# A hybrid encoder layer on one core: a weight unit's low part last in the projections, the first squares pinned in SP's order, the last sums made in order of use

## The chip, the core and the metric

The kernel runs on one core of a Trainium2 chip, as one program with one launch. Five engines work side by side: TensorE (PE, matmuls, with its weight loads listed as PEld), VectorE (DVE), ScalarE (ACT), GpSimd (POOL) and SyncE (SP). In this kernel SP issues most of the loads, POOL's queue the loads that add to what is already there, ACT's queue a few others. The metric is the device time of one execution in microseconds. Three executions of the kernel before took 2008.85, 2009.45 and 2011.46 us; the median, 2009.45 us, is the time before. Times "at 53.19" are microseconds from the start of the span of one profiled execution.

## The reference, cut to what matters

A layer works on 512 tokens of 2048 channels in float32:

```python
xn = rms_norm(x, attn_norm_g)
u_val, u_gate, q, k, v = split(xn @ w_in)            # 2048 -> 1024 + 1024 + 3 * 1024
y_conv = silu(layer_norm(depthwise_conv(u_val * sigmoid(u_gate), 31 taps)))
y_na = neighborhood_attention(q, k, v, rpb)          # 16 heads of 64, 8 x 64 grid, window 8 x 16
mixed = concat(rms_norm(y_conv, conv_out_g), rms_norm(y_na, na_out_g))
x = x + mixed @ w_out                                # 2048 -> 2048
xn = rms_norm(x, ffn_norm_g)
gate, val = split(depthwise_conv(xn @ w_up, 3 taps)) # 2048 -> 2 * 5632
x = x + (silu(gate) * val) @ w_down                  # 5632 -> 2048
out = rms_norm(x, final_norm_g)
```

## The kernel before, in words

**Three matmuls for one.** The matmuls run on a reduced float32 type (fp32r), and each operand is a sum of a high and a low part. A weight unit is a tile of 128 x 1024 elements (512 KB), which serves 8 contraction steps (k) of 128. SP loads it into `raw`; ScalarE copies it, rounded, into `whi` (line 125); VectorE subtracts that from `raw`, and the rest is `wlo` (line 126). There are four buffers each for `whi` and `wlo`. The input x, transposed, is split in the same way into `xh` and `xl`, with the first norm's gain (`split_x`). `mm3` (lines 135 to 142) makes the three matmuls of one k: high by high, high by low (the input's low part), low by high, so line 142 is the first to read `wlo`, two matmuls after line 138 first reads `whi`.

**Order of the work.** The program is written as one list of weight units, `plan`. `weights()` hands out the next one, and sees to it that loads and splits of the three units behind it (`AHEAD`) have been written down by then. A scheduler (Tile) then orders the instructions of each engine by priority, which is mostly the place in the program; `shifted` moves an operation's priority, `issue_after` and `behind` tie it to another, and `pin` (`keep_in_program_order`) fixes the written order among pinned instructions of an engine. Work that goes between (statistics, attention) is written as generators, the `steps`; `tick` runs one step of them after each unit's matmuls.

**The stages.** First come the projections: eight channel blocks of the convolution group ("a" in `ORDER`), each a gate and a value block of two units each (`glu`, `project`), and eight head pairs ("q") of q, k and v blocks. The first block (`first_glu`) interleaves gate and value, matmul triple by matmul triple, in two PSUM banks; its weights come in small pieces (`piece`, `early`), pinned in order with the loads of x. `stats1` makes the first norm's factor beside this: it loads the untransposed x (`xn`) as eight tiles of 512 KB, ScalarE squares and sums each (line 306), VectorE reduces (line 310), a diagonal matrix is made, a matmul with ones (`st`, line 237) broadcasts it, and ScalarE copies the result out as `rstd` (line 239). The tiles of `xn` share the nine buffers of `raw`. In `gated` VectorE multiplies the gate block by `rstd` (line 352), ScalarE applies the sigmoid, VectorE makes the product, and 31 taps of the depthwise convolution follow on VectorE (line 363 the first, line 367 the other thirty), with a priority 600 later, so that they fill VectorE's free time.

The output projection has two halves of 16 columns, one for each group. The second half's `after` (from line 599) takes each finished column from PSUM: VectorE multiplies by the group's norm (line 602) and adds to x (`x2`), `sum_sq` adds its square to `acc2`, four transposes on TensorE (line 594, `turned`) prepare a copy for the end. After every second column the pair is scaled by the second norm's gain (line 611, tiles `b`, whose quarters are b11, b12, b21, b22) and made into seven operands (`halves`: a high part by ScalarE, line 586, and a low part by VectorE).

The up projection (44 hidden tiles) and the down projection then use a Strassen-like scheme of seven products, taken in the orders `TURN` and `TURN2`. In the up projection's `product` (line 696) the eight high matmuls of a unit, 512 columns wide, come first and the eight low ones, 256 wide, after them; product 2 uses `mm3` at 256 columns. Each finished hidden tile runs through `hidden` (among it the tile `vl`, line 710, and a SiLU). The down projection's `product2` takes a unit of weights and one operand and feeds four PSUM banks in turn with three matmuls each (lines 821 to 823); the last four units (`TAIL`) are fed bank by bank, so that the banks end one after the other.

Of the kernel before, what the change touches and what calls it, by code (L numbers as in the profile page):

```python
# [16 lines left out]
P = 128  # L17
# [55 lines left out]
def layer(ctx: ExitStack, tc: tile.TileContext, xT, xn, w_in, w_out, w_up, w_down, par, tab, g3, out):  # L73
# [70 lines left out]

    steps, asteps = [], []
# [137 lines left out]
    for k in range(U, KD):  # L283
        last = split_x(k)
    last = pin(nc.sync.dma_start(prm, par))
    for i in range(4):
        plan.append(lambda i=i: early[i])
# [6 lines left out]
    del plan[4:8]  # L294
# [5 lines left out]
    def stats1():  # L300
        part = sm.tile([P, S // P, 2], F32, tag="ss", name="ss")
        for t in range(S // P):
            for i in range(2):
                x = t4([P, D // 2], "xn")
                nc.sync.dma_start(x, xn[t * P:(t + 1) * P, i * D // 2:(i + 1) * D // 2])
                nc.scalar.activation(x, x, AF.Square, accum_out=part[:, t, i:i + 1])
            if t < S // P - 1:
                yield
        sums = sm.tile([P, S // P], F32, tag="s1", name="s1")
        nc.vector.tensor_reduce(sums, part, axis=AX.X, op=ALU.add)  # L310
        rstd.append((yield from root_steps(sums, D, "rstd1")))
# [287 lines left out]
    def after(d, ps):  # L599
# [4 lines left out]
        sum_sq(acc2, x2[d], d == 0)  # L604
        turned(d)
        if d % 2 == 0:
            return
        b = []
        for i in (d - 1, d):
            t = t2("b")  # L610
            nc.scalar.activation(t, x2[i], AF.Copy, scale=pc("g2", i))
            b += [t[:, :H], t[:, H:]]
        b11, b12, b21, b22 = b
        t = t2("t")
        t1, t2_ = t[:, :H], t[:, H:]
        nc.vector.tensor_sub(t1, b11, b12)
        nc.vector.scalar_tensor_tensor(t2_, b22, -1.0, t1, op0=ALU.mult, op1=ALU.subtract)
        t = t2("t")
        t3, t4_ = t[:, :H], t[:, H:]
        nc.vector.tensor_sub(t3, b22, b12)  # L620
        nc.vector.scalar_tensor_tensor(t4_, t2_, -1.0, b21, op0=ALU.mult, op1=ALU.subtract)
        for c in TURN:
            halves((t4_, t1, t3, b11, t2_, b21, b22)[c], c)


# [6 lines left out]
    def stats2():  # L632
        rstd2.append((yield from rsqrt_steps(acc2, D, "rstd2")))

# [50 lines left out]
    def up(f, done):  # L685

        def product(c, ps, more):
# [5 lines left out]
            else:  # L693
                for part, n in ((hi, S), (lo, H)):
                    for k in range(U):
                        i = nc.tensor.matmul(ps[:, :n], part[:, k * P:(k + 1) * P], comb[c][k][:, :n],  # L696
                                             start=part is hi and k == 0 and not more,
                                             stop=part is lo and k == U - 1, skip_group_check=more)
                        if part is hi and k == 0 and tight:
                            pin(i)  # L700
# [113 lines left out]
    def product2(c, ps, more):  # L814

        def feed(w, h, i, start, stop):
            wh, wl = w
            t, d = divmod(i, Q)
            t, d = slice(t * P, (t + 1) * P), slice(d * S, (d + 1) * S)
            tl = slice(H + t.start, H + t.stop)  # L820
            nc.tensor.matmul(ps[i], h[:, t], wh[:, d], start=start and not more, stop=False, skip_group_check=more)  # L821
            nc.tensor.matmul(ps[i], h[:, t], wl[:, d], start=False, stop=False, skip_group_check=more)  # L822
            return nc.tensor.matmul(ps[i], h[:, tl], wh[:, d], start=False, stop=stop, skip_group_check=more)  # L823
# [178 lines left out]
```

## Time and profile before

| | |
|---|---|
| median of three runs | 2009.45 us (2008.85 to 2011.46) |
| the profiled execution | 2008.65 us |
| its span in the trace | 2006.9 us |
| mean granted TensorE clock | 0.997 |
| PE busy | 1985.5 us, 99%, 10525 matmuls |
| VectorE busy | 1598.5 us, 80% |
| ScalarE busy | 1095.9 us, 55% |
| GpSimd busy | 225.8 us, 11% |
| DMA | 451.01 MB, mean 225 GB/s |

The page's second table cuts the span in 40 slices of about 50 us each and gives the busy share of each engine in tenths:

```profile
PE   9999999999999999999999999999999999999998
DVE  4994899488556888888888888888888898886765
ACT  6234433447534666566666666566666644554654
```

The projections take the first eleven slices or so, the output projection ends in the fifteenth, the down projection begins in the thirty-second. TensorE shows 9 in all slices but the last.

How to read the other lines: a row of the groups has line, engine, operation, tile written <- tiles read, partitions x elements, count, then the busy time in us and the mean of one in ns, then the engine's idle time just ahead of such instructions and what ended most of it. A matmul's duration there (389 ns) is from its start to its modelled end; matmuls overlap, and the time that one adds to the engine is the distance between starts. A row of the timeline has the start, the busy time, the engine, the line, the operation and its tiles, how many stand in the row, and in brackets the wait just ahead of it and what ended it. A row of the waits has the waiting engine, tile and line, the engine and tile it waited for, the sum in us, the number of waits and the longest. A row of the windows has the stretch and its length in us, the busy time (and number of instructions) of PE, PEld, DVE, ACT and POOL, the granted TensorE clock, the busy share of the DMA engines and the GB/s that they moved.

### The profile page before, as it was taken

The numbers are of one execution on the slowest core, as the hardware profiler recorded it, in microseconds if no ns is written. First come the engines' busy times: TensorE is split into PE (matmuls) and PEld (weight loads), VectorE is DVE, ScalarE is ACT, GpSimd is POOL, SyncE is SP. The second block draws the span as 40 slices with busy tenths as digits, with TensorE's granted clock in tenths as the row PEclk, the third lists the DMA queues.
The fourth block names the chain that finished last, engine by engine and source line by source line (L and its number), as shares of the span: only waits on it lengthen the run. The fifth ranks groups of instructions, "written<-read, shape, count | busy, mean of one in ns | idle before, by whom it ended". The sixth has DMA issues, their size and how long they took to land.

```text
span 2006.9 us, 28334 instructions
## 1 busy us (share of the span) xinstructions
PE 1985.5 (99%) x10525; PEld 1688.0 (84%) x10525; DVE 1598.5 (80%) x2296; ACT 1095.9 (55%) x1728; POOL 225.8 (11%) x310
## 2 busy tenths in 40 slices
PE   9999999999999999999999999999999999999998
PEld 7778888887788889888898988898898888888886
DVE  4994899488556888888888888888888898886765
ACT  6234433447534666566666666566666644554654
POOL 0111111111001111111111111111110400000000
PEclk9999999999999999999999999999999999999999
DMA  9677767766858888989999999999997877666563
GB/s 352 158 197 180 177 172 190 192 182 166 296 147 206 214 213 230 271 237 260 249 260 247 261 252 253 258 250 262 250 246 200 335 254 235 216 217 191 191 213 110
DMA packets 143115, 451.01 MB, mean 225 GB/s; under 512 B 15232, under 2 KB 23936, under 8 KB 141568
## 3 DMA queue, kind: packets, MB, share of 16 engines
q1 hardware_dynamic: 90608, 293.98, 43.0%
q0 software_dynamic: 42624, 148.92, 34.7%
q10 hardware_dynamic: 9744, 6.30, 1.0%
q8 instruction: 82, 1.34, 0.3%
q14 instruction: 57, 0.47, 0.1%
HBM read 430.27 MB, written 111.15 MB: 270 GB/s over the span
## 4 chain that ended last, share of the span: by engine, by line
PE 96%; DVE 2%; ACT 1%; DMA 1%; issue 0%; SPq 0%; DVEq 0%; ACTq 0%
PE pu L696 37%; PE pd L821 7%; PE pd L822 7%; PE pd L823 7%; PE pj L138 7%; PE pj L141 7%; PE pj L142 7%; PE po L138 3%; PE po L141 3%; PE po L142 3%; PE pu L141 2%; PE pu L142 2%; PE pu L138 2%; DVE y L367 1%; PE po L495 1%; PE sc L453 1%
## 5 line engine op out<-in xcount | busy, mean ns | idle before, releaser
L125 ACT ACTIVATE whi<-raw 128x1024 fp32r<-128x1024 f32 x572 | 605.4, 1059 | 709.7 <-PE pj L141 220.4
L126 DVE TENSOR_TENSOR wlo<-raw,whi 128x1024 fp32r<-128x1024 f32 x572 | 698.7, 1222 | 285.2 <-ACT whi L125 261.1
L696 PE MATMUL pu<-xc,whi 128*128 128x512 f32 x2112 | 529.8, 392 | 0.2 <-ACT pu L706 0.2
L696 PEld LDWEIGHTS pu<-xc,whi 128*128 128x128 f32 x2112 | 379.9, 189 | 68.8 <-issue 0.5
L696 PEld LDWEIGHTS pu<-xc,wlo 128*128 128x128 f32 x2112 | 288.1, 190 | 20.5
L696 PE MATMUL pu<-xc,wlo 128*128 128x256 f32 x2112 | 294.5, 282 | 0.0
L142 PE MATMUL pj<-xh,wlo 128*128 128x512 f32 x624 | 244.7, 392 | 7.1 <-DVE wlo L126 7.1
L138 PE MATMUL pj<-xh,whi 128*128 128x512 f32 x624 | 247.5, 399 | 0.0
L141 PE MATMUL pj<-xl,whi 128*128 128x512 f32 x624 | 245.0, 393 | 0.1
L821 PE MATMUL pd<-whi,ho 128*128 128x512 f32 x616 | 239.7, 389 | 0.5 <-DVE vl L710 0.5
L822 PE MATMUL pd<-wlo,ho 128*128 128x512 f32 x616 | 239.8, 389 | 0.0
L823 PE MATMUL pd<-whi,ho 128*128 128x512 f32 x616 | 239.5, 389 | 0.0
L367 DVE SCALAR_TENSOR_TENSOR y<-ch,prm,y 128x509 f32<-128x509 f32 (+14 forms) x240 | 170.0, 740 | 3.2
L142 PEld LDWEIGHTS pj<-xh,wlo 128*128 128x128 f32 x624 | 118.0, 189 | 33.0 <-DVE wlo L126 8.0
L138 PEld LDWEIGHTS pj<-xh,whi 128*128 128x128 f32 x624 | 118.0, 189 | 28.4 <-issue 3.7
L141 PEld LDWEIGHTS pj<-xl,whi 128*128 128x128 f32 x624 | 117.8, 189 | 24.3 <-issue 0.7
L821 PEld LDWEIGHTS pd<-whi,ho 128*128 128x128 f32 x616 | 115.7, 188 | 25.0 <-DVE vl L710 0.9
L823 PEld LDWEIGHTS pd<-whi,ho 128*128 128x128 f32 x616 | 115.7, 188 | 24.1
L822 PEld LDWEIGHTS pd<-wlo,ho 128*128 128x128 f32 x616 | 115.7, 188 | 24.1 <-DVE wlo L126 0.3
L194 POOL DMA_DIRECT2D ws<-in_w_down x88 | 79.4, 902 | 495.8 <-DMA ws<-ws 254.8
L643 POOL DMA_DIRECT2D raw<-in_w_up x88 | 86.1, 979 | 408.2 <-ACT vl L709 133.1
L138 PE MATMUL pu<-xc,whi 128*128 128x256 f32 x352 | 99.8, 284 | 1.4 <-ACT xc L586 1.4
(185 smaller groups left out, 2526.0 us busy)
## 6 DMA issues: line engine op xcount, KB each, us to landing
raw<-in_w_up SPq DMA_DIRECT2D x220, 512.0 KB, 7.2
ws<-in_w_down POOLq DMA_DIRECT2D x132, 512.0 KB, 7.4
raw<-in_w_up POOLq DMA_DIRECT2D x88, 512.0 KB, 8.5
raw<-ws SPq DMA_DIRECT2D x88, 512.0 KB, 3.4
raw<-in_w_in SPq DMA_DIRECT2D x78, 512.0 KB, 4.8
raw<-in_w_down SPq DMA_DIRECT2D x66, 512.0 KB, 4.2
ws<-ws POOLq DMA_DIRECT2D x44, 512.0 KB, 7.5
raw<-in_w_out SPq DMA_DIRECT2D x32, 512.0 KB, 4.9
```

The lines of the kernel that those rows point to most:

```text
L125: i = nc.scalar.activation(hi[:, :n], raw[:, :n], AF.Copy)
L126: j = nc.vector.tensor_sub(lo[:, :n], raw[:, :n], hi[:, :n].bitcast(F32))
L138: i = nc.tensor.matmul(ps, hi[:, a], mh, start=start, stop=False, skip_group_check=more)
L141: nc.tensor.matmul(ps, hi[:, a], ml, start=False, stop=False, skip_group_check=more)
L142: return nc.tensor.matmul(ps, lo[:, a], mh, start=False, stop=stop, skip_group_check=more)
L194: nc.gpsimd.dma_start(wsum[c][k], w_down[k, {1: A21, 2: A11, 4: A11, 6: A12}[c]], accum_op=ALU.add, max_dma_last_dim=ROW)
L367: nc.vector.scalar_tensor_tensor(y[:, a:b], h[:, a + j - PAD:b + j - PAD], prm[:, o + j:o + j + 1], y[:, a:b], op0=ALU.mult, op1=ALU.add)
L643: nc.gpsimd.dma_start(a[c], w_up[f, q2], accum_op=ALU.add)
L696: i = nc.tensor.matmul(ps[:, :n], part[:, k * P:(k + 1) * P], comb[c][k][:, :n], start=part is hi and k == 0 and not more, stop=part is lo ...
L821: nc.tensor.matmul(ps[i], h[:, t], wh[:, d], start=start and not more, stop=False, skip_group_check=more)
L822: nc.tensor.matmul(ps[i], h[:, t], wl[:, d], start=False, stop=False, skip_group_check=more)
L823: return nc.tensor.matmul(ps[i], h[:, tl], wh[:, d], start=False, stop=stop, skip_group_check=more)
```

## The change

It has four parts.

1. In `project` and in `out_half` a new helper, `group`, takes the place of `mm3`: the sixteen matmuls of a unit that read `whi` (high by high and high by low for each of 8 k) come first, the eight that read `wlo` last. In the up projection one product of one hidden tile (`f == 0 and c == 3`, the first) gets its sixteen matmuls sorted by k, high and low in turn; all others stay.
2. The two units of the second gate block, and the eight loads of `xn` with their squares, are written down at the head of the program, pinned, in a fixed order: unit, four tiles of `xn`, unit, four tiles of `xn`. The load of the parameters (`prm`) is pinned behind them instead of ahead. `stats1` keeps three empty steps and then reduces.
3. In `after`, for every pair of columns, the scaling by the gain comes straight behind the addition, each of the seven operands is made in the order in which the first products use them (3, 2, 4, 5, 1, 0, 6), directly behind the sum that it needs, and squares and transposes of the pair come behind. The transposes run for two columns at a time, one column later than before, and the last column's move into `stats2`.
4. In the down projection `feed` goes through a unit's twelve matmuls by kind: high by high for the four banks, then the operand's low part by high for the four banks, then the low weights for the four banks, so each matmul writes another bank than the one ahead of it. The last four units are fed per bank, by kind over the four units.

The diff, cut to its core:

```diff
+    def group(ps, ws, ms, first, last):
+
+        for k, ((hi, _, wk), (mh, ml)) in enumerate(zip(ws, ms)):
+            hi = hi[:, wk * P:(wk + 1) * P]
+            nc.tensor.matmul(ps, hi, mh, start=first and k == 0, stop=False)
+            nc.tensor.matmul(ps, hi, ml, start=False, stop=False)
+        for k, ((_, lo, wk), (mh, _)) in enumerate(zip(ws, ms)):
+            i = nc.tensor.matmul(ps, lo[:, wk * P:(wk + 1) * P], mh, start=False, stop=last and k == len(ws) - 1)
+        return i
...
-        last = split_x(k)
+        split_x(k)
+    squares = sm.tile([P, S // P, 2], F32, tag="ss", name="ss")
+    for u in range(2):
+        raw, i = raw_unit(w_in[NC_ + 1, :, u * U * P:(u + 1) * U * P], U * P)
+        pin(i)
+        for t in range(2 * u, 2 * u + 2):
+            for i in range(2):
+                x = t4([P, D // 2], "xn")
+                pin(nc.sync.dma_start(x, xn[t * P:(t + 1) * P, i * D // 2:(i + 1) * D // 2]))
+                if t == 2 * u and i == 0:
+                    w = parts(raw, U * P)
+                    pin(w[2])
+                    pin(w[3])
+                    early.append(w[:2])
+                pin(nc.scalar.activation(x, x, AF.Square, accum_out=squares[:, t, i:i + 1]))
     last = pin(nc.sync.dma_start(prm, par))
-    for i in range(4):
+    for i in range(len(early)):
...
-    del plan[4:8]
+    del plan[6:12]
...
     def stats1():
-        part = sm.tile([P, S // P, 2], F32, tag="ss", name="ss")
-        for t in range(S // P):
...
+        for _ in range(3):
+            yield
...
-            for k in range(U):
-                kk = u * U + k
-                m = mm3(ps, w, k, xs[kk][0], xs[kk][1], kk == 0, kk == KD - 1)
+            m = group(ps, [(*w, k) for k in range(U)], xs[u * U:(u + 1) * U], u == 0, u == KD // U - 1)
...
-            for k in range(U):
-                i = mm3(ps, w, k, m[k][0], m[k][1], k == 0, k == U - 1)
+            i = group(ps, [(*w, k) for k in range(U)], m, True, True)
...
-        sum_sq(acc2, x2[d], d == 0)
-        turned(d)
+        t = t2("b")
+        nc.scalar.activation(t, x2[d], AF.Copy, scale=pc("g2", d))
+        bs[d % 2] = t[:, :H], t[:, H:]
         if d % 2 == 0:
             return
...
+        halves(b11, 3)
+        nc.vector.tensor_sub(t3, b22, b12)
+        halves(t3, 2)
         nc.vector.tensor_sub(t1, b11, b12)
         nc.vector.scalar_tensor_tensor(t2_, b22, -1.0, t1, op0=ALU.mult, op1=ALU.subtract)
-        t = t2("t")
...
+        halves(t2_, 4)
+        halves(b21, 5)
+        halves(t1, 1)
         nc.vector.scalar_tensor_tensor(t4_, t2_, -1.0, b21, op0=ALU.mult, op1=ALU.subtract)
...
+        halves(t4_, 0)
+        halves(b22, 6)
+        for i in (d - 1, d):
+            sum_sq(acc2, x2[i], i == 0)
+        for i in (d - 2, d - 1):
+            if i >= 0:
+                turned(i)
...
         rstd2.append((yield from rsqrt_steps(acc2, D, "rstd2")))
+        turned(KD - 1)
...
-                for part, n in ((hi, S), (lo, H)):
-                    for k in range(U):
...
+                turns = [(part, n, k) for part, n in ((hi, S), (lo, H)) for k in range(U)]
+                if f == 0 and c == 3:
+                    turns.sort(key=lambda a: a[2])
...
-        def feed(w, h, i, start, stop):
...
+        def feed(got, banks, start, stop):
+
+            for kind in range(3):
+                for i in banks:
+                    t, d = divmod(i, Q)
+                    d = slice(d * S, (d + 1) * S)
+                    for j, ((wh, wl), h) in enumerate(got):
+                        o = H if kind == 1 else 0
+                        w = wl if kind == 2 else wh
+                        m = nc.tensor.matmul(ps[i], h[:, o + t * P:o + (t + 1) * P], w[:, d],
...
         for j in range(n):
-            w, h = weights()
-            for i in range(2 * Q):
-                m = feed(w, h, i, j == 0, j == NK - 1)
-            tick(m)
+            tick(feed([weights()], range(2 * Q), j == 0, j == NK - 1))
...
             for i in range(2 * Q):
-                for j, (w, h) in enumerate(got):
-                    feed(w, h, i, False, j == NK - n - 1)
+                feed(got, [i], False, True)
```

More of the change, by code (lines that the diff above doesn't have):

```diff
@@ L300, in stats1 @@
     def stats1():
-        part = sm.tile([P, S // P, 2], F32, tag="ss", name="ss")
-        for t in range(S // P):
[L303 to L308, printed above, removed]
+        for _ in range(3):
+            yield
         sums = sm.tile([P, S // P], F32, tag="s1", name="s1")
-        nc.vector.tensor_reduce(sums, part, axis=AX.X, op=ALU.add)
+        nc.vector.tensor_reduce(sums, squares, axis=AX.X, op=ALU.add)
         rstd.append((yield from root_steps(sums, D, "rstd1")))
```

36 lines of the change are left out of this document (12 added, 24 removed).

## The prediction

> **What bounds the kernel now.** I read the page first, then the waits, then windows and the order of time at each place where TensorE (PE) stood still.
>
> ```profile
> span 2006.9 us, 28334 instructions
> PE 1985.5 (99%) x10525; PEld 1688.0 (84%) x10525; DVE 1598.5 (80%) x2296; ACT 1095.9 (55%) x1728; POOL 225.8 (11%) x310
> L142 PE MATMUL pj<-xh,wlo 128*128 128x512 f32 x624 | 244.7, 392 | 7.1 <-DVE wlo L126 7.1
> ...
> L821 PE MATMUL pd<-whi,ho 128*128 128x512 f32 x616 | 239.7, 389 | 0.5 <-DVE vl L710 0.5
> ...
> L823 PE MATMUL pd<-whi,ho 128*128 128x512 f32 x616 | 239.5, 389 | 0.0
> ```
> ```profile
> PE pj L142 <- DVE wlo L126: 7.1, 2, 3.8
> ```
>
> TensorE is busy for 99% of the span, so only its stalls and its extra work can be won or lost. The waits put 7.1 us on two places, both in the projections, both a low part (`wlo`) that VectorE had not yet written. In order of time:
>
> ```profile
> 51.83 0.39 PE L138 MATMUL pj<-xh,whi 128*128 128x512 f32 x1
> ...
> 53.19 0.39 PE L138 MATMUL pj<-xh,whi 128*128 128x512 f32 x1
> ...
> 57.16 0.50 PE L142 MATMUL pj<-xh,wlo 128*128 128x512 f32 x1 [3.35 <-DVE wlo L126]
> ...
> 61.83 0.40 PE L138 MATMUL pj<-xh,whi 128*128 128x512 f32 x1
> ```
> ```profile
> 101.99 0.39 PE L138 MATMUL pj<-xh,whi 128*128 128x512 f32 x1
> ...
> 106.38 0.80 PE L142 MATMUL pj<-xh,wlo 128*128 128x512 f32 x1 [3.78 <-DVE wlo L126]
> ...
> 109.80 0.40 PE L141 MATMUL pj<-xl,whi 128*128 128x512 f32 x1
> ```
> ```profile
> 7.30:30.50 23.20, 22.45 (x94) 17.12 (x93) 15.93 (x23) 18.26 (x28) 0.00 (x0) 1.00 1.03 392
> 57.16:61.90 4.74, 4.74 (x14) 3.74 (x15) 4.74 (x6) 0.00 (x0) 0.00 (x0) 0.64 0.45 131
> 106.40:109.70 3.30, 3.30 (x8) 2.62 (x9) 3.30 (x4) 0.00 (x0) 0.00 (x0) 0.52 0.62 186
> 713.10:714.55 1.45, 0.08 (x2) 0.02 (x1) 1.28 (x4) 0.93 (x4) 0.92 (x1) 1.00 0.74 253
> ```
>
> From 51.83 to 53.19 are 6 matmuls: 0.2267 us each. From 53.19 to 61.83 are 15 (3.40 us) in 8.64 us, so 5.24 us are lost; from 101.99 to 109.80 are 10 (2.27 us) in 7.81 us, 5.54 us lost. That is 10.78 us and not 7.1: the windows (the third column from the right is the granted clock) show 0.64 and 0.52 just after each stall. The 1.37 us stall at 713 was granted 1.00. So a long wait is paid about one and a half times, a short one once.
>
> **The change, part by part.** First, the squares. The parameter load (336 KB) and one 512 KB unit move on SP's queue from ahead of the last square's load to behind it.
>
> ```profile
> 24.41 1.06 ACT L125 ACTIVATE whi<-raw 128x1024 fp32r<-128x1024 f32 x1 [1.40 <-DMA raw<-in_w_in]
> ...
> 32.33 1.06 ACT L125 ACTIVATE whi<-raw 128x1024 fp32r<-128x1024 f32 x1 [0.28 <-DMA raw<-in_w_in]
> ```
> ```profile
> 38.61 0.16 DVE L310 TENSOR_REDUCE s<-ss 128x4 f32<-128x8 f32 x1 [3.96 <-ACT xn L306]
> ...
> 41.12 1.22 DVE L126 TENSOR_TENSOR wlo<-raw,whi 128x1024 fp32r<-128x1024 f32 x1
> 47.18 0.69 DVE L352 TENSOR_TENSOR gate<-pj,rstd 128x512 f32<-128x512 f32 x1 [4.84 <-ACT rstd L239]
> ```
> ```profile
> 45.65 0.87 PE st L237 x2
> ```
>
> Between the two landings lie six loads of 512 KB: 1.32 us each. So the last square lands 2.2 us earlier, its sum comes at about 36.6 instead of 38.61, the diagonal at 39.1 instead of 41.1. In the built order of the changed kernel the broadcast matmul (`st`) stands behind 48 matmuls of the second gate pair instead of 66: those begin where the window 7.30:30.50 above ends, so it runs at 30.5 + 48 x 0.2267 = 41.4, 2.3 us after its diagonal, not at 45.65. `rstd` and with it the gates are 4.2 us earlier: 42.9 for 47.18. What lies behind it now: the third and fourth units of that pair are needed at 42.3 and 47.7 and land, after squares and parameters, at about 37.5 and 38.9.
>
> Second, the low parts last. Units of 24 matmuls (5.44 us) follow each other from 53.19 in both kernels. A low part is then needed 16 matmuls (3.63 us) into its unit, not after 2.
>
> ```profile
> 55.89 2.35 DVE L126 TENSOR_TENSOR wlo<-raw,whi 128x1024 fp32r<-128x1024 f32 x2
> 58.16 0.73 DVE L367 SCALAR_TENSOR_TENSOR y<-ch,prm,y 128x501 f32<-128x501 f32 x1
> ...
> 82.49 9.29 DVE L367 SCALAR_TENSOR_TENSOR y<-ch,prm,y 128x509 f32<-128x509 f32 x14
> 91.69 0.69 DVE L419 TENSOR_TENSOR q<-pj,rstd 128x512 f32<-128x512 f32 x1
> 92.29 7.94 DVE L367 SCALAR_TENSOR_TENSOR y<-ch,prm,y 128x502 f32<-128x502 f32 x12
> ...
> 105.10 2.36 DVE L126 TENSOR_TENSOR wlo<-raw,whi 128x1024 fp32r<-128x1024 f32 x2
> ```
>
> From start to start a tap costs 0.655 us (9.20 for 14), a multiplication 0.60, a split 1.135 (2.27 for 2). First stall: the gates' chain ahead of the split begins 4.2 us earlier and holds one operation less, so the split starts at about 51.3 for 55.89 and ends at 52.5; needed at 56.8. The stall goes (between 0 and, if only the order changed, 0.3 us).
>
> Second stall: VectorE works without pause from 64 to 105 and stays late. In the new order it starts the split of the sixth unit when the second has been read (four buffers), 53.19 + 2 x 5.44 + 0.2 = 64.3. From there to the split that stalled stand 3 splits, 44 taps, 5 multiplications and one first tap (0.45): 3.4 + 28.8 + 3.0 + 0.45 = 35.65. The split runs from 99.95 to 101.2. TensorE asks for it in its ninth unit, 53.19 + 8 x 5.44 + 3.63 = 100.34. A wait of 0.9 us remains, 1.05 us with the slower restart, and by the row at 713.10 no clock is lost. Bounds: 0 and the 5.54 us of before; I take 1.05, the queue being added up from this very stretch. Gain of both: 10.78 - 1.05 = 9.7 us. In the other projections the low part was never waited for, so there the order is worth 0. High parts are read out 8 matmuls earlier, which frees ScalarE only.
>
> Third, the hand-over to the up projection.
>
> ```profile
> 712.88 0.28 PE L142 MATMUL pu<-xc,wlo 128*128 128x256 f32 x1
> 714.53 0.39 PE L138 MATMUL pu<-xc,whi 128*128 128x256 f32 x1 [1.37 <-ACT xc L586]
> ...
> 717.05 0.28 PE L142 MATMUL pu<-xc,wlo 128*128 128x256 f32 x1
> 717.49 2.11 PE L696 MATMUL pu<-xc,whi 128*128 128x512 f32 x8 [0.17 <-ACT pu L706]
> ```
> ```profile
> 707.98 0.69 DVE L602 TENSOR_TENSOR oa<-po,rna 128x512 f32<-128x512 f32 x1
> ```
> ```profile
> 712.52 0.71 ACT L611 ACTIVATE b<-x,prm 128x512 f32<-128x512 f32 x1
> ```
>
> A 256-column matmul steps 0.12, so 1.53 and 0.32 are lost: 1.85 us. Afterwards, counted from the last output matmul: VectorE multiplies at 0.9 (a prepared sum of weights holds it that long), splits weights to 2.7, adds to 3.4, ScalarE scales to 4.1, VectorE subtracts, ScalarE and VectorE make the pair's first operand (`b11`) by 5.0. TensorE, with 8 transposes (0.9), 3 clearing matmuls (0.7), 7 high and low pairs sorted by k (2.4) and 5 short matmuls (0.6), asks at 4.9. The squares now stand behind these: `acc2` is ready at 10.4, its matmul is due at 10.5; the diagonal at 13.9 is due at 15.2. I leave 0.2 us: gain 1.65, bounds 0 (a new wait as long as the old) and 1.85.
>
> Fourth, the transposes of the second output half go in pairs.
>
> ```profile
> 634.41 0.60 PE L594 MATMUL trx<-ident,x 128*128 128x128 f32 x4
> ...
> 646.42 0.60 PE L594 MATMUL trx<-ident,x 128*128 128x128 f32 x4
> ```
> ```profile
> 123.63 0.40 PE L142 MATMUL pj<-xh,wlo 128*128 128x512 f32 x1
> 123.87 1.04 PE L441 MATMUL trv<-ident,vw 128*128 128x128 f32 x8
> ...
> 124.98 0.39 PE L141 MATMUL pj<-xl,whi 128*128 128x512 f32 x1
> ```
>
> A pair of columns lasts 12.01 us, 48 matmuls of it 10.88: two groups of 4 cost 1.13. Eight transposes in a row behind a finished unit cost 1.35 - 2 x 0.2267 = 0.9. Over 7 pairs that is 1.6 us; bounds 0 and 1.7. I take 1.6.
>
> Fifth, the down projection: the same 1848 matmuls, each in another bank than the one ahead. L821 always came behind a change of bank, L823 never: 389 ns both, so 0. The wait at its start (0.5 by L821) stays. The built order puts a weight split ahead of the last hidden tile's activation there, which I price at 0.2 us lost, up to 1.1. [...]
>
> Sum: 9.7 + 1.65 + 1.6 - 0.2 = 12.75 us. The profiled execution took 2008.65 us (1.75 beside its span), so 1995.9; the median of the three runs is 0.8 above it, 2009.45, and gives **1996.7**.
>
> **The rivals.**
> (a) The squares come no earlier, since SP's issues wait for free buffers. Then the split at 55.89 still meets its 56.8 nearly, but VectorE's queue begins 4.6 us later and loses its pauses: the second low part comes at about 103.9, 3.5 us late, long enough for the half clock of 106.40 (1.6 us). Against it: ScalarE waited for these loads by DMA at 24.41 and 32.33, so transfer order rules. 9.7 falls to 5.7: 2000.7.
> (b) The wait stays short, but the scheduler's other orders bring one or two new ones in attention or at the down projection's start, 2 to 3 us: 1999.5. For it: ScalarE's and VectorE's orders shift everywhere a little.
> (c) The other side: changing bank at every matmul costs. It would need 12.75 us / 1848 = 7 ns a matmul to eat the gain, and 9 ns to be slower by 4 us: 2013. Against it stand L821's 389 ns.
> [...]
>
> **How the numbers follow.** Forecast 0.78, (a) 0.08, (b) 0.07, (c) 0.03, (d) 0.01, and 0.03 for a gain of which only the last parts hold (2005 to 2009). 0.2% (4 us) is what a measurement here can tell. The forecast's own range: from 1994.6 (no wait left, all upper gains, and the runs' scatter of 0.6) to 1999.0 (second wait of 2 us, no gain from transposes). With (a), (b) and the runs' scatter (the slowest is 2.0 over the median, of which I take 1.3): 1994.5 to 2002.0. Faster 0.92, within 0.2% 0.04, slower 0.04.
>
> **What would show it.** The chain must hold `rstd` at 42 to 43, no wait near 53 to 57, one wait near 100 of under 1.5 us with the clock at 1.00 behind it; pairs of output columns at 11.78 us; no wait over 0.4 us in the up projection's first 10 us; down projection matmuls at 389 ns. Wrong would make it: `rstd` past 45, a `wlo` wait over 3 us, or a granted clock under 1.00 after 1580.

## The result, and the profile after

The changed kernel takes 1994.59 us (median of six executions, 1994.55 to 1995.20); the kernel before, run beside it, 2009.49 us (2008.85 to 2014.89). The ratio, into which every execution of both goes (their means are 1994.74 and 2010.55 us), is 0.9921, with a 95% interval of 0.9909 to 0.9934: faster, by 14.9 us from median to median. The forecast was 1996.7. The median lies at the very edge of the stated range (1994.5 to 2002.0), and the median before times the ratio, 1993.6, lies below it: the gain was larger than forecast, and larger than the range allowed for.

From the page of the changed kernel, the lines that answer to those of before:

```profile
span 1992.8 us, 28315 instructions
PE 1979.3 (99%) x10525; PEld 1685.3 (85%) x10525; DVE 1596.1 (80%) x2296; ACT 1097.6 (55%) x1728; POOL 225.7 (11%) x310
L846 PE MATMUL pd<-whi,ho 128*128 128x512 f32 x1232 | 305.1, 389 | 0.5 <-DVE vl L731 0.5
L152 PE MATMUL pj<-xh,wlo 128*128 128x512 f32 x608 | 150.4, 389 | 0.8 <-DVE wlo L126 0.8
```

TensorE has as many matmuls as before and is busy 6.2 us less; of 7.1 us of waits on low parts in the projections 0.8 is left. The places where it stood still, in order of time (ScalarE, VectorE and TensorE of the changed kernel):

```profile
42.40 0.60 ACT L249 ACTIVATE rstd<-st 128x512 f32<-128x512 f32 x1 [1.94 <-PE st L247]
```
```profile
43.02 0.69 DVE L368 TENSOR_TENSOR gate<-pj,rstd 128x512 f32<-128x512 f32 x1 [1.12 <-ACT rstd L249]
...
51.71 1.22 DVE L126 TENSOR_TENSOR wlo<-raw,whi 128x1024 fp32r<-128x1024 f32 x1
...
64.25 1.23 DVE L126 TENSOR_TENSOR wlo<-raw,whi 128x1024 fp32r<-128x1024 f32 x1 [1.14 <-ACT whi L125]
...
99.97 2.35 DVE L126 TENSOR_TENSOR wlo<-raw,whi 128x1024 fp32r<-128x1024 f32 x2
```
```profile
56.74 1.52 PE L152 MATMUL pj<-xh,wlo 128*128 128x512 f32 x6
...
100.04 0.39 PE L150 MATMUL pj<-xl,whi 128*128 128x512 f32 x1
101.23 2.11 PE L152 MATMUL pj<-xh,wlo 128*128 128x512 f32 x8 [0.81 <-DVE wlo L126]
```

`rstd` comes at 42.40 and the gates begin at 43.02, not at 47.18. The first low part is ready at 52.9 (51.71 and 1.22 us of work) and read at 56.74: no wait. The second is read at 101.23, 1.19 us behind the matmul ahead of it, which is 0.97 more than a step of 0.2267. The granted clock is 1.00 from 4.8 us to the last 5 us of the span.

A way to place the gain is to take the matmul with the same number, counted from the start, in both profiled executions. Rows at the borders of units and stages, start in us (the last row is the end of the span):

```
matmul   before    after   earlier by   what lies between it and the row above
   240    63.91    58.56      5.35      first low-part stall
   480   123.87   114.06      9.80      second low-part stall
  2040   434.35   424.56      9.79      projections, attention
  2880   599.42   588.97     10.45      last projections, first output half
  3720   765.81   751.80     14.01      second output half, hand-over, first up units
  8640  1571.05  1557.04     14.01      up projection
  9000  1651.25  1637.50     13.75      down projection's start
 10440  1977.65  1963.90     13.75      down projection
   end  2006.89  1992.81     14.08      last units, norm, writes
```

### The profile page after: what moved, and what is told of

It is laid out like the page before. It is cut to its first block, busy times and chain, and to the rows that moved or that the text cites. A ratio compares the mean times of both kernels' runs of the same rounds, so it can differ in the third digit from the quotient of the medians.

```text
span 1992.8 us, 28315 instructions
## 1 busy us (share of the span) xinstructions
PE 1979.3 (99%) x10525; PEld 1685.3 (85%) x10525; DVE 1596.1 (80%) x2296; ACT 1097.6 (55%) x1728; POOL 225.7 (11%) x310
## 4 chain that ended last, share of the span: by engine, by line
PE 96%; DVE 2%; DMA 1%; ACT 0%; issue 0%; SPq 0%; DVEq 0%; ACTq 0%
PE pu L718 37%; PE pd L846 21%; PE pj L149 7%; PE pj L152 7%; PE pj L150 7%; PE po L149 3%; PE po L150 3%; PE po L152 3%; PE pu L142 2%; PE pu L141 2%; PE pu L138 2%; DVE y L383 1%; PE sc L469 1%; PE po L511 1%; PE trp L497 1%; DMA raw<-in_w_in 0%
## 5 line engine op out<-in xcount | busy, mean ns | idle before, releaser
L846 PE MATMUL pd<-whi,ho 128*128 128x512 f32 x1232 | 305.1, 389 | 0.5 <-DVE vl L731 0.5
L718 PE MATMUL pu<-xc,wlo 128*128 128x256 f32 x2112 | 295.6, 282 | 0.0
L149 PE MATMUL pj<-xh,whi 128*128 128x512 f32 x608 | 241.5, 397 | 0.0
L150 PE MATMUL pj<-xl,whi 128*128 128x512 f32 x608 | 237.7, 391 | 0.0
L383 DVE SCALAR_TENSOR_TENSOR y<-ch,prm,y 128x510 f32<-128x510 f32 (+14 forms) x240 | 169.8, 739 | 3.1
L846 PE MATMUL pd<-wlo,ho 128*128 128x512 f32 x616 | 165.0, 389 | 0.0
L152 PE MATMUL pj<-xh,wlo 128*128 128x512 f32 x608 | 150.4, 389 | 0.8 <-DVE wlo L126 0.8
L152 PEld LDWEIGHTS pj<-xh,wlo 128*128 128x128 f32 x608 | 114.0, 188 | 24.9 <-DVE wlo L126 1.2
L138 PE MATMUL pu<-xc,whi 128*128 128x256 f32 x352 | 99.6, 283 | 0.0
L142 PE MATMUL pu<-xc,wlo 128*128 128x256 f32 x352 | 99.6, 283 | 0.0
L141 PE MATMUL pu<-xc,whi 128*128 128x256 f32 x352 | 99.6, 283 | 0.0
```

The source lines that it names most:

```text
L138: i = nc.tensor.matmul(ps, hi[:, a], mh, start=start, stop=False, skip_group_check=more)
L141: nc.tensor.matmul(ps, hi[:, a], ml, start=False, stop=False, skip_group_check=more)
L142: return nc.tensor.matmul(ps, lo[:, a], mh, start=False, stop=stop, skip_group_check=more)
L149: nc.tensor.matmul(ps, hi, mh, start=first and k == 0, stop=False)
L150: nc.tensor.matmul(ps, hi, ml, start=False, stop=False)
L152: i = nc.tensor.matmul(ps, lo[:, wk * P:(wk + 1) * P], mh, start=False, stop=last and k == len(ws) - 1)
```

## The experiments

The theory: TensorE's two stalls come from VectorE's lateness; the pinned squares start VectorE's queue 4.2 us earlier, the new order gives each low part 14 matmuls more, and only both together take the stalls away. The rivals: one of the two alone does it; the gain is elsewhere.

### The low parts last, alone

The kernel before with `group` in `project` and `out_half`:

```diff
-            for k in range(U):
-                kk = u * U + k
-                m = mm3(ps, w, k, xs[kk][0], xs[kk][1], kk == 0, kk == KD - 1)
+            m = group(ps, [(*w, k) for k in range(U)], xs[u * U:(u + 1) * U], u == 0, u == KD // U - 1)
```

> The kernel before with the low parts last in the two projections alone. If VectorE's lateness and the place of the low part together set the two stalls (my theory): the broadcast matmul stands behind 70 matmuls of the second gate pair, at about 46.4, so rstd comes later than before, the first split ends near 57.9 and is asked for at 56.8: a wait of about 1.1 us; the second low part comes at about 104.7 and is asked for at 101.5: a wait of about 3.2 us with up to 1.6 us of half clock behind it. Of 10.8 us about 4.9 are won: 4.9 us faster than before. If the order alone is what removes the stalls (rival): no wait over 0.5 us at either place, 10.8 us faster. If the order does nothing without the squares: both waits stay over 3 us, less than 1 us faster. Transposes and hand-over stay as before.

Measured: 2006.16 us against 2010.25, 4.1 us less, ratio 0.998 (0.9971 to 0.9989). Its TensorE rows at the two places:

```profile
58.37 1.88 PE L152 MATMUL pj<-xh,wlo 128*128 128x512 f32 x7 [0.41 <-DVE wlo L126]
...
106.28 0.97 PE L152 MATMUL pj<-xh,wlo 128*128 128x512 f32 x3 [4.10 <-DVE wlo L126]
```

The first wait is short, the second is as long as before (4.1 us; 3.2 were expected), with a granted clock of 0.50 behind it (107.50 to 110.80, last section). By matmul 480 this kernel is 3.15 us ahead of the kernel before, not 9.8: the order alone isn't enough, and it does something. The rest was not expected: 0.70 us are won between matmuls 1900 and 2600, while the hand-over wait is longer than before (1.8 us for 1.4) and the transposes ahead of it wait 0.9 us; 1.0 us is lost between 2880 and 3720.

### The squares first, alone

The kernel before with the pinned units, loads and squares, and the parameters behind them.

> The kernel before with the pinned first loads and squares alone. My theory: rstd at 42 to 43, the first wait gone (split ready near 52.9, asked for at 53.6); the second low part is ready near 101 but asked for at 97.2, two matmuls into its unit: a wait of about 3.8 us with up to 1.6 us of half clock: 5.4 us faster than before, the second stall as large as before. Rival, the earlier squares are what counts and the order only rearranges: both waits under 1.5 us, 9 to 11 us faster. Rival, the squares come no earlier: rstd past 45, no gain.

Measured: 2003.54 us against 2010.25, ratio 0.9958 (0.9943 to 0.9973). Windows of this kernel around its one low-part stall, and two later ones (columns as in the windows above: stretch and length, busy time of PE, PEld, DVE, ACT, POOL, granted clock, DMA share, GB/s):

```profile
97.20:100.50 3.30, 1.06 (x5) 0.57 (x4) 3.30 (x5) 1.06 (x1) 0.24 (x1) 1.00 0.77 127
100.55:103.90 3.35, 3.35 (x9) 2.59 (x8) 3.35 (x5) 0.00 (x0) 0.00 (x0) 0.50 0.88 221
701.30:704.60 3.30, 1.67 (x10) 1.49 (x11) 3.30 (x5) 1.58 (x3) 0.04 (x1) 1.00 0.00 0
```

The first stall is gone, the second is a wait of 2.2 us with a granted clock of 0.50 behind it (second row, 3.35 us). By matmul 480 the kernel is 6.06 us ahead. 3.8 us were expected for the second wait: between the sixth unit's split and this one stand 41 taps and 4 multiplications in VectorE's queue here, and I had counted the 44 and 5 of the changed kernel. With the run above: 3.15 and 6.06 make 9.2 of the 9.8 us that both together bring. So the two gains nearly add up; neither part alone takes both stalls away, but only 0.6 us of the gain needs them together. In this execution 2.5 us are lost again near 703 (third row); that wait has its own run below.

### The sums in order of use, alone

The kernel before with the new `after`, `turned(KD - 1)` in `stats2` and the sorted product.

> The kernel before with the sums in order of use, the paired transposes and the one sorted product alone. My theory: both low-part waits in the projections as before; a pair of output columns lasts 11.78 instead of 12.01 us (1.6 us over seven pairs); no wait over 0.2 us in the first 10 us of the up projection instead of 1.4 and 0.2 (1.85 us): 3.5 us faster. Rival, the squares put behind the sums make a new wait as long as the old at the second norm's matmul: 1.6 us faster, with 1 to 2 us of wait on acc2.

Measured: 2005.73 us against 2010.25, ratio 0.9972 (0.9961 to 0.9983). In the trace the hand-over wait on `xc` is gone; one of another kind is left:

```profile
PE pu L703 <- ACT pu L712: 0.4, 1, 0.4
```

From matmul 2880 to 3720 it gains 3.25 us, what the prediction's third and fourth step summed to (1.65 and 1.6), and the changed kernel gains 3.56, without that 0.4 us wait. The low-part waits are those of before (7.1 us), as expected. What they cost is not: by matmul 480 this execution is 1.29 us behind the kernel before; its mean granted clock is 0.996, that of the kernel before 0.997. Its seven executions lie within 2.0 us (2004.87 to 2006.87); those of the runs with one of the other parts alone spread over 4.7, 4.7 and 7.9 us.

### Each matmul in another bank, alone

> The kernel before with the down projection's matmuls by kind, each in another bank, alone. My theory: matmuls stay at 389 ns and start every 0.2267 us, granted clock 1.00 throughout the stage, total within 0.5 us of before. Rival, changing bank costs 7 ns a matmul: 13 us slower. [...]

Measured: 2010.05 us against 2010.25, ratio 0.9993 (0.9983 to 1.0004). From matmul 9000 to 10440 both kernels take 326.40 us. A group and a window of its page:

```profile
L825 PE MATMUL pd<-whi,ho 128*128 128x512 f32 x1232 | 305.1, 389 | 0.5 <-DVE vl L710 0.5
```
```profile
1600.00:1990.00 390.00, 390.00 (x1722) 323.03 (x1721) 301.47 (x496) 205.59 (x307) 3.23 (x6) 1.00 0.65 212
```

Changing the bank at each matmul costs nothing here, and the clock stays at 1.00. 0.25 us are lost at the stage's start, as in the changed kernel. From median to median the four parts alone gain 4.1, 6.7, 4.5 and 0.2 us, 15.5 in sum, and all four together 14.9.

### The transposes one column at a time

The changed kernel with

```diff
         if d % 2 == 0:
+            if d:
+                turned(d - 1)
             return
...
-        for i in (d - 2, d - 1):
-            if i >= 0:
-                turned(i)
+        turned(d - 1)
```

> The changed kernel with its transposes made for one column at a time again, one column late. If the pairing is what shortened the columns (my theory): a pair of output columns lasts 12.01 us for 11.78, the span is 1.6 us longer than the changed kernel's, nothing else moves by over 0.2 us. Rival, the columns are shorter because of the order of high and low parts around them: 11.78 stays, no difference.

Measured, in one execution: 1997.57 us, span 1995.8, 3.0 us over the changed kernel's, but not where it was expected. Rows of TensorE, of this kernel first, then of the changed kernel and of the kernel before:

```profile
630.46 0.60 PE L609 MATMUL trx<-ident,x 128*128 128x128 f32 x4
630.81 0.48 PE L149 MATMUL po<-mbh,whi 128*128 128x512 f32 x1
...
642.28 0.60 PE L609 MATMUL trx<-ident,x 128*128 128x128 f32 x4
```
```profile
635.70 1.03 PE L609 MATMUL trx<-ident,x 128*128 128x128 f32 x8
636.49 0.48 PE L149 MATMUL po<-mbh,whi 128*128 128x512 f32 x1
...
647.48 0.71 PE L609 MATMUL trx<-ident,x 128*128 128x128 f32 x5
```
```profile
636.93 0.40 PE L138 MATMUL po<-mbh,whi 128*128 128x512 f32 x1
637.31 0.63 PE L594 MATMUL trx<-ident,x 128*128 128x128 f32 x4
637.70 0.47 PE L141 MATMUL po<-mbl,whi 128*128 128x512 f32 x1
...
646.42 0.60 PE L594 MATMUL trx<-ident,x 128*128 128x128 f32 x4
646.78 0.48 PE L138 MATMUL po<-mbh,whi 128*128 128x512 f32 x1
```

Two columns take 11.82 us here (630.46 to 642.28), 11.78 in pairs, 12.01 before. So the pairing is worth 0.04 us and the place 0.19: four transposes between two units delay the next matmul by 0.36 us (646.42 to 646.78, or 630.46 to 630.81); in the midst of a unit, behind a high matmul and ahead of one that reads the same weights, a group costs 0.54 (0.77 from 636.93 to 637.70, less a step of 0.2267). The 3 us are lost later. Two waits of 0.9 us stand between 690 and 730 us. The earlier one, and the rows of ScalarE, VectorE and TensorE that lead to it:

```profile
PE pu L703 <- DVE oa L617: 0.9, 1, 0.9
```
```profile
694.65 0.42 ACT L601 ACTIVATE xc<-b 128x256 fp32r<-128x256 f32 x1 [1.58 <-DMA xt<-xt]
...
696.23 0.69 DVE L617 TENSOR_TENSOR oa<-po,rna 128x512 f32<-128x512 f32 x1
...
696.97 0.50 PE L703 MATMUL pu<-xc 128*128 128x512 f32 x1 [0.86 <-DVE oa L617]
```

ScalarE waits 1.58 us to write an operand (`xc`), until the write of a transposed column (`xt`) to DRAM is done; VectorE, which needs that operand's high part, stands still for 1.02 us; it takes the last column but one from PSUM only at 696.23, and TensorE waits 0.86 us for that. The changed kernel has no such wait of `xc`. It is the wait that has its own run below; whether the place of the transposes brings it on, one execution can't tell. What else makes up the 3 us (eight transposes fill TensorE there in the changed kernel, here four, elsewhere; the second wait stands at 721.71, on the first hidden tile) no run here separates. So the 3 us can't be read as the price of transposes that aren't paired.

### The first product unsorted

```diff
-                if f == 0 and c == 3:
+                if False:
```

> The changed kernel with the first up product unsorted (eight high matmuls, then eight low ones). My theory: the last k's operand is asked for 0.6 us earlier than it is ready: a wait of 0.4 to 0.7 us on xc at the hand-over, span longer by as much. Rival, the order of the sums alone removes the wait: no difference over 0.1 us.

Measured, in one execution: 1994.32 us, span 1992.5. Between matmuls 2880 and 3720 it is 0.02 us slower than the changed kernel. The rival was right. The matmul that needs the late operand is the same and starts at nearly the same time (699.29, and 699.42 in the changed kernel); ahead of it the scheduler put twelve short matmuls of the next product instead of five:

```profile
697.63 0.28 PE L138 MATMUL pu<-xc,whi 128*128 128x256 f32 x1
...
699.29 0.50 PE L718 MATMUL pu<-xc,whi 128*128 128x512 f32 x1
```

### Buffers of their own for the transposed columns

The kernel before, on one chip, scattered from 2007.84 to 2015.85 us in 22 executions; the changed kernel stays within 0.65 us. The traces of the squares alone and of the banks alone, both with the old `after`, show a wait that the profiled execution of before doesn't have; of the one with the banks alone, TensorE and ScalarE between 690 and 720 us:

```profile
PE trx L594 <- DVE x L603: 2.0, 1, 2.0
```
```profile
ACT xc L586 <- DMA xt<-xt: 2.3, 1, 2.3
```

An operand (`xc`) that ScalarE wants to write waits for the write of a transposed column (`xt`) to DRAM; behind it VectorE's queue, and the next transposes, stand still. Both tiles come from one pool of 75 buffers. The run takes four of them for `xt` alone:

```diff
-NT = 75
+NT = 71
...
-        r = t2("xt").rearrange("p (t k) -> p t k", t=S // P)
+        r = tp.tile([P, S], F32, tag="xt", name="xt", bufs=4).rearrange("p (t k) -> p t k", t=S // P)
```

> The kernel before with four buffers of their own for the transposed columns xt, taken from the pool that they shared with the operands xc (75 to 71 buffers). If the 2 us wait of the transposes near 705, which some executions of the kernel before show and its profiled one doesn't, comes from an xc that takes over a buffer which the write of xt is still reading (my theory): no wait of ScalarE on that write and none of over 0.3 us by the transposes, and the median 0.5 to 2 us under that of the kernel before, with fewer executions over 2012. Rival, VectorE or ScalarE is late there for another reason: the wait shows again, median within 0.5 us.

Measured: 2008.71 us against 2009.83, ratio 0.999 (0.9982 to 0.9998). Its twelve executions lie between 2007.03 and 2009.90, the seventeen of before between 2008.32 and 2016.95. Eight of the seventeen are over 2010, none of the twelve. Neither wait is in its trace, which alone shows little, since the one trace of before doesn't have them either. The times bear the theory out: 1.1 us of the median and the executions over 2010 go with the shared buffers. How many executions of the kernel before meet that wait can't be read, since only one has a trace. A scatter of 2.9 us stays. One source of it shows in the traces: the low-part stalls don't cost the same in each, with waits of the same length (7.1 us, the longest 3.8, in this trace and in that of before); the second one costs 0.9 us more in this run's trace.

### Where 0.66 us in attention come from

The changed kernel with the low parts last in the first 20 units only; the later units of the projections go k by k again (the output projection, against what the text below says, was left as changed).

```diff
+            if weights.at < 20:
+                m = group(ps, [(*w, k) for k in range(U)], xs[u * U:(u + 1) * U], u == 0, u == KD // U - 1)
+            else:
+                for k in range(U):
+                    kk = u * U + k
+                    m = mm3(ps, w, k, xs[kk][0], xs[kk][1], kk == 0, kk == KD - 1)
```

> The changed kernel with the low parts last only as far as the unit that waited at 101 (20 units); the later projection units and the output projection's first and second half take high and low parts k by k again. My reading of the 0.66 us between 445 and 505 that the sum did not foresee: they come from the later units' order, so the two 0.5 us waits (st on s, trp on s) return and the span is 0.5 to 0.9 us longer, the first 110 us unchanged. Rival, they come from the earlier squares and shorter queue of taps: nothing changes before 600 us, within 0.2 us.

Measured: 1995.54 us, ratio 0.9921 (0.9903 to 0.9938). Two waits of the kernel before are back in its list; first the list of before, then that of this run:

```profile
PE trp L481 <- ACT s L469: 0.5, 1, 0.5
...
PE st L382 <- DVE s L461: 0.5, 1, 0.5
```
```profile
PE trp L502 <- ACT s L490: 0.5, 1, 0.5
...
PE st L403 <- DVE s L482: 0.5, 1, 0.5
```

Between matmuls 1900 and 2600 it loses 0.68 us to the changed kernel, and behind matmul 480 nothing elsewhere. The gain there belongs to the order of the later units.

### A version with an early split

The wait that is left at 101.2 is VectorE's queue of taps, so a version takes taps from ahead of that split: its unit is written down one unit earlier, and pinned ahead of the third block's taps. Two small edits at the down projection's start go with it (the operand's low part third in six units, and the free second bank of a tile kept).

```diff
+        if len(made) == 16:
+            pin(j)
...
-        while len(made) < min(at + 1 + AHEAD, len(plan)):
+        while len(made) < min(at + 1 + AHEAD + (at == 12), len(plan)):
...
-            nc.vector.tensor_scalar(y, h, ...)
+            first = nc.vector.tensor_scalar(y, h, ...)
+            if i == 2:
+                pin(first)
...
-            for kind in range(3):
+            for kind in kinds:          # (0, 2, 1) in the first six units, else range(3)
...
-    a = four(True)
+    a = [two[:, 0], two[:, 1]] + [psa.tile([P, S], F32, tag="tr", name="pd", bufs=2) for _ in range(2)]
```

> The changed kernel with three small edits: the weights of the unit whose low part is still waited for at 101.2 are written down one unit earlier, and its split is pinned on VectorE ahead of the third block's taps; the down projection's first bank group keeps the tile whose second bank is free, so that six more matmuls can run ahead of the bank that waits for the last hidden tile; in the first six units there the operand's low part is read third, not second. If VectorE's queue of taps sets the remaining wait in the projections (my theory): no wait over 0.2 us near 100, 1.1 us won; at the down projection's start the 0.64 and 0.19 us stalls go: 1.9 us less than the changed kernel, a span of about 1990.9. Rival, the wait only moves: taps held back make VectorE late for a later unit, a wait of 1 us or more between 100 and 130, no gain.

Measured: 1993.02 us, ratio 0.9913 (0.9899 to 0.9926), span 1990.8. VectorE of this version:

```profile
80.11 1.22 DVE L126 TENSOR_TENSOR wlo<-raw,whi 128x1024 fp32r<-128x1024 f32 x1
```

The split runs at 80.1 instead of 99.97, the matmuls that read it begin at 99.75, the wait is gone (1.10 us between matmuls 400 and 480), and nothing waits in its place. At the down projection's start 0.26 us are won by the new order; the 0.64 us stall stays: the spare bank didn't help. Another 0.52 us lie before 33 us, in the first loads, which none of the edits touches; that the span came out as expected is luck. So the version ran once more, beside the changed kernel:

> The version with the early split once more, on the same chip as the changed kernel: 1.4 us (its gains near 101 and at the down projection's start) to 2 us under the changed kernel's median. If the gain seen was scatter of the first loads: within 0.5 us.

> The changed kernel once more, beside the version with the early split and the kernel before. The same span as before within 0.6 us (1992.2 to 1993.4), executions within 1 us of each other, about 15 us under the kernel before; the kernel before again scatters over 5 us or more.

Measured: 1993.42 us (1992.77 to 1993.72) against 1994.67 (1993.88 to 1995.08) of the changed kernel, 1.25 us less; both against 2009.89 (2009.47 to 2017.63) of the kernel before, ratios 0.9909 (0.9892 to 0.9927) and 0.9916 (0.9900 to 0.9931). 1.4 were expected as the least: 0.13 us are lost at the hand-over, by a 0.2 us wait on `xc` that the first execution of this version didn't have. No execution of this version took as long as the shortest of the changed kernel. It beats both kernels, the changed one by little. The changed kernel's own span is 1992.9 us, as expected, its executions lie within 1.2 us (1 was expected), and those of before scatter over 8 us again.

## Why the prediction failed, and what of it held

**What failed.** The mechanism of the two stalls held; the sum around it was too small, and its range too narrow below. Two steps failed. The first is a term put at nothing: "In the other projections the low part was never waited for, so there the order is worth 0." It is worth 0.66 us. The second is the step from the profile to the median: "the median of the three runs is 0.8 above it, 2009.45, and gives 1996.7." It gave the changed kernel the scatter of the kernel before, and the runs showed that this scatter goes with the change. The range's lower end counted all upper gains of the named terms and the scatter, and nothing for what wasn't named. Of the 3.1 us between 1996.7 and 1993.6, the terms of the sum are 1.3, the carried distance 0.8, and 1.0 the slower executions of the kernel before that ran beside the changed one.

**The sum, step by step**, forecast against the same matmul's start in both traces: the two low-part stalls 9.7, measured 9.80. Hand-over and second output half 1.65 + 1.6 = 3.25, measured 3.56 (1.77 and 1.79, divided at matmul 3380, the first of the up projection). The down projection's start -0.2, measured -0.26. Last projections and attention 0, measured 0.66. The last units and writes 0, measured 0.33. The sum was 12.75 and is 14.08.

**First and second step: right, in place and size.** The broadcast was put at 41.4 and runs at 41.34; the gates were put at 42.9 and begin at 43.02; the split of the first stall was put at 51.3 and starts at 51.71; the sixth unit's split at 64.3, it starts at 64.25; the late split at 99.95, it starts at 99.97; the wait at 0.9, 1.05 with the restart, and it is 0.97 and 0.11. The queue could be added up so closely because VectorE has no pause between the last two splits. The clock stayed at 1.00. The runs with one part alone bear the two steps out: 3.15 and 6.06 us, and 0.6 us more with both.

**The term of 0.** The premise holds, the conclusion doesn't. With the order of a unit, what the scheduler puts between its matmuls moves too, and two waits of 0.5 us on the attention's results went. They stood in the list of waits of before; I had costed only the waits on low parts. The run with k by k in the later units shows that they belong to this order.

**Third step: right in its reading of the wait, 0.12 us too small.** The wait went as worked out. The 0.2 us kept back shrank to 0.15 us, a wait of the second norm's matmul (`st` on `acc`). But the sort by k, which I had counted as the reason that TensorE asks later, is worth 0.02 us: the scheduler fills the time with other matmuls.

**Fourth step: right in the length of a pair, wrong in its reason.** The columns last 11.78 us as forecast; but not because transposes go in pairs. They went from the midst of a unit to its end. I counted seven pairs, 1.6 us, and put 1.7 as the upper bound; the whole half gains 1.79.

**Fifth step: right.** No cost of the banks, and a small stall at the start, on the low part of an operand (`ho`). TensorE's weight load waits for it, and ScalarE's rows there give a reason why it is late:

```profile
PEld pd L846 <- DVE ho L800: 0.3, 1, 0.3
```
```profile
1567.87 1.06 ACT L125 ACTIVATE whi<-raw 128x1024 fp32r<-128x1024 f32 x1 [2.88 <-PE pd L846]
1568.83 0.80 ACT L760 ACTIVATE uy<-g,prm 128x512 f32<-128x512 f32 x1
```

The weight split (1567.87) stands ahead of the last hidden tile's activation (`uy`), as the forecast said; VectorE has one more split there too, at 1568.96. The operand's low part is made at 1572.75, 1.3 us later against the matmuls than in the kernel before, and asked for only two matmuls later. That the splits make it late is read from the order of the rows; no run here moves them.

**The last part: not in the sum.** 0.33 us at the end: 0.17 of it in the last units by kind (the run with the banks alone has the same 0.17), the rest behind the last instruction of ScalarE, in the landing of the last write; from that instruction to the end of the span it is 4.5 to 5.1 us in the traces here, in no order by kernel.

**The scale to the median.** I added the 0.8 us by which the median of three stood over the profiled execution to the forecast too. But the profiled execution of before was one of its fast ones. Beside the changed kernel, the mean of before (2010.55) is another 1.1 us over its median, with one execution at 2014.89; the executions of the changed kernel lie within 0.65 us, and its profiled one (1994.58) is at their median. Two sources of scatter show in the runs, and neither shows in the traces of the changed kernel: the wait on the shared buffers (1.1 us of the median, by the run with buffers of their own; of the four parts alone only the sums in order of use have executions close together), and the low-part stalls, which with the same 7.1 us of waits cost 0.9 us more (buffers of their own) and 1.29 us more (sums in order of use) than in the trace of before. ScalarE of the changed kernel still waits once for a write of `xt` (0.6 us), but TensorE does not wait behind it. That the two are all of the scatter isn't shown.

**The rivals.** (a) was excluded by `rstd` at 42.40. (b) brought no new waits; those of the scheduler's other orders went the other way. (c) fell: the matmuls stayed at 389 ns. (d), a lowered clock in the down projection, shows in no trace or run: in the window of the run with the banks alone, 1600 to 1990, the granted clock is 1.00 and TensorE busy for 390.00 us of 390.00, and in the changed kernel's trace the clock is 1.00 up to 1987.9.

## What to carry to other kernels

A split that stays late can be found by adding up the queue of the engine that makes it: the starts of its operations, from the last pause on, gave the new wait to within 0.1 us here. Where an order changes inside every unit, look at all waits in the list, also those on other tiles, since whatever is placed between the units moves with it. And where a kernel's executions scatter while others agree within 0.1%, the one trace you have may lack a wait, or show one that costs more in another (0.9 and 1.29 us more here): ask which part of the scatter the change removes, count it as a gain of its own rather than carry the distance to the median over, and let the range hold it.

## What the runs showed of the hardware

**The granted clock behind the stalls.** In the trace of the kernel before, the granted clock was 0.50 from 58.39 to 61.80 and from 106.17 to 109.59, 3.41 us each, and 1.00 between the two. The first began 1.2 us behind the end of a wait of 3.35 us (57.16), the second 0.2 us ahead of the end of one of 3.78 us (106.38). Behind the wait of 1.37 us that ended at 714.53 it stayed at 1.00, and behind that of 0.81 us in the changed kernel (to 101.23) too. Windows of the kernel with the banks alone (the last holds the wait on `xt` of the run above), and of that with the low parts last alone:

```profile
52.50:55.80 3.30, 1.37 (x7) 0.79 (x5) 3.30 (x6) 3.16 (x4) 0.94 (x1) 1.00 0.49 78
55.90:59.20 3.30, 1.97 (x5) 1.58 (x6) 3.30 (x5) 0.00 (x0) 0.00 (x0) 0.50 0.42 76
59.30:62.70 3.40, 3.40 (x10) 2.62 (x9) 3.40 (x5) 0.00 (x0) 0.00 (x0) 0.50 0.74 190
707.90:711.20 3.30, 1.57 (x9) 1.43 (x10) 3.30 (x5) 1.48 (x3) 0.00 (x0) 1.00 0.00 0
```
```profile
104.10:107.40 3.30, 1.12 (x5) 0.94 (x6) 3.30 (x5) 1.06 (x1) 0.00 (x0) 1.00 0.04 10
107.50:110.80 3.30, 3.30 (x9) 2.51 (x9) 3.30 (x4) 0.00 (x0) 0.51 (x1) 0.50 0.84 259
```

The rows at 52.50 and 104.10, and at 97.20 of the run with the squares, have 1.93, 2.18 and 2.24 us idle (length less PE's busy time), and 0.50 behind them. The rows at 707.90, and at 701.30 of the run with the squares, have 1.73 and 1.63 us idle; the matmuls behind them start 0.23 us apart (seven from 711.48 to 713.07 and from 704.78 to 706.38), the step at full clock, where those behind the first stall of before started 0.43 us apart (58.43 to 61.41) at 0.50. The length of a wait alone didn't decide here: 2.24 us ahead of 100.18 had 0.50 behind it, 2.34 us ahead of 702.93 in the same trace had not. Nor did 0.50 last equally long: 3.41 us in the kernel before, through both rows from 55.90 to 62.70 in that with the banks alone, with waits of the same length (7.1 us, the longest 3.8) in both; at matmul 240 the kernel with the banks alone is 1.0 us behind the kernel before. What decides when the clock falls and for how long isn't shown by so few cases.

**Four transposes in the midst of a unit** cost 0.54 us, at its end 0.36 (rows above); why, no run here tells.
